# Batch norm over 64 tiles: loads of tiles 1 to 63 move from SyncE's queue to GpSimd's software queue, as one packet for each DMA engine

## The chip, the cores and the metric

The kernel runs on one core of a Trainium2 chip. The metric is the device time of one execution, in microseconds (us); the time of a kernel is the median of its runs. A profile is one execution recorded by the hardware profiler; its span is the time from its first to its last recorded event. The core has 16 DMA engines, which move data between the chip's main memory (HBM) and the core's on-chip buffer (SBUF, 128 partitions). Engines that issue or compute are named PE (TensorE), DVE (VectorE), ACT (ScalarE), POOL (GpSimd) and SP (SyncE); "SPq" and "ACTq" are the instruction queues of SP and ACT, from which DMAs are issued.

## The reference

The kernel computes an inference batch norm: each of 256 channels is scaled and shifted by constants of its own.

```python
# x: (32, 256, 128, 128) float32; gamma, beta, running_mean, running_var: (256,)
gamma * (x - mean) / np.sqrt(var + 1e-5) + beta     # each parameter as (1, 256, 1, 1)
```

x and the output are 536.87 MB each. There is one multiplication and one addition for each element that is read and written.

## The kernel before

A tile is 128 channels of one image: 128 partitions of 16,384 float32, that is 64 KB a partition and 8.39 MB in all. There are 64 tiles (`NT`), taken in order through three buffers (`NBUF`): tile i lives in buffer i % 3. A DMA of a whole tile is spread over all 16 DMA engines, eight partitions (rows of 64 KB) for each.

The parameters are fetched in four small DMAs (line 91) into `rows`, turned with a transpose and four copies on DVE, and made into `scale_t` and `shift_t` (lines 107 to 125). They are done once, at the start.

For each tile the work is split by columns: DVE does columns 0 to 14,336 (`VCOLS`), in a first piece of 2,560 (`STEP`) and a second of 11,776; ACT does the remaining 2,048. The last tile is split at 9,216 (`VLAST`). Tile 0 arrives in two halves of 8,192 columns (lines 88 and 95), and DVE's two pieces of it are 8,192 and 6,144 columns.

All order is written out by hand with semaphores, in one critical section; no scheduler moves anything:

- Loads are issued by SP (line 102). For i of 3 and more, SP first waits until the store of tile i - 3 is complete (`stored`, line 101), since that frees the buffer, and then until DVE has finished the first piece of tile i - 1 (`vdone`, line 104). So there is one load in flight at a time once the first three are through.
- DVE waits for the load of tile i (`loaded`, through `landed`) ahead of its first piece. `vdone` counts its pieces, two for each tile.
- ACT waits until both pieces of tile i are done, then until the store of tile i - 1 is complete, works on its columns (line 141), and issues the store of tile i on its own queue (line 154). So there is one store in flight at a time, up to the last two: ACT's part of the last tile waits for its load and not for the store before.
- SP ends with waits for the last store of each buffer (line 172). POOL issues nothing of the kernel's; it sets four constants before it starts.

`loaded` has one semaphore for each buffer, and every DMA adds 16 to its semaphore when it is complete. `landed(i)` gives the semaphore and the value that mean that tile i is there.

Of the kernel before, what the change touches and what calls it, by code (L numbers as in the profile page):

```python
# [8 lines left out]
NBUF = 3  # L9
# [7 lines left out]
@with_exitstack  # L17
def kernel(
    ctx: ExitStack,
    tc: tile.TileContext,  # L20
    x: bass.AP,
    gamma: bass.AP,
    beta: bass.AP,
    running_mean: bass.AP,
    running_var: bass.AP,
    out: bass.AP,
):
    nc = tc.nc
    eps = 1e-5
    f32 = mybir.dt.float32  # L30

    N, C, H, W = x.shape
    P = nc.NUM_PARTITIONS
    assert C % P == 0
    NCB = C // P
    HW = H * W
    NT = N * NCB
    B = 32
    NQ = P // B
    NE = 16  # L40
    NPAR = 4

    xr = x.rearrange("n (cb p) h w -> (n cb) p (h w)", p=P)
    outr = out.rearrange("n (cb p) h w -> (n cb) p (h w)", p=P)

    params = ctx.enter_context(tc.tile_pool(name="params", bufs=1))
    data = ctx.enter_context(tc.tile_pool(name="data", bufs=1))
    bufs = [data.tile([P, HW], f32, name=f"t{s}", tag=f"t{s}") for s in range(NBUF)]
    rows = params.tile([B, NPAR * C], f32, name="rows", tag="rows")
    turned = params.tile([B, NPAR * C], f32, name="turned", tag="turned")  # L50
    par = params.tile([P, NPAR, NCB], f32, name="par", tag="par")
    eps_t = params.tile([P, 1], f32, name="eps_t", tag="eps")
    std_t = params.tile([P, NCB], f32, name="std_t", tag="std")
    rstd_t = params.tile([P, NCB], f32, name="rstd_t", tag="rstd")
    scale_t = params.tile([P, NCB], f32, name="scale_t", tag="scale")
    ms_t = params.tile([P, NCB], f32, name="ms_t", tag="ms")
    shift_t = params.tile([P, NCB], f32, name="shift_t", tag="shift")

    loaded = [tc.alloc_semaphore(f"loaded{s}") for s in range(NBUF)]
    stored = [tc.alloc_semaphore(f"stored{s}") for s in range(NBUF)]
    early = tc.alloc_semaphore("early")
    vdone = tc.alloc_semaphore("vdone")
    adone = tc.alloc_semaphore("adone")
    fetched = tc.alloc_semaphore("fetched")
    vec = tc.alloc_semaphore("vec")
    act = tc.alloc_semaphore("act")

    with tc.tile_critical():  # L70
        count = [0]

        def step(inst, sem=None, value=None):

            if sem is not None:
                inst._wait_ge(sem, value)
            elif count[0]:
                inst._wait_ge(vec, count[0])
            inst.then_inc(vec, 1)
            count[0] += 1  # L80
            return count[0]

        left, right = slice(0, HW // 2), slice(HW // 2, HW)
        last = NT - 1

        nc.sync.dma_start(out=bufs[0][:, left], in_=xr[0][:, left]).then_inc(early, 16)
        zeroed = step(nc.vector.memset(rows[:], 0.0))  # L89
        for r, ap in enumerate((running_var, gamma, beta, running_mean)):  # L90
            inst = nc.sync.dma_start(out=rows[0:NE, r * C : (r + 1) * C], in_=ap.partition_broadcast(NE))  # L91
            if r == 0:
                inst._wait_ge(vec, zeroed)
            inst.then_inc(fetched, 16)
        nc.sync.dma_start(out=bufs[0][:, right], in_=xr[0][:, right]).then_inc(loaded[0], 16)  # L95
        for i in range(1, NT):
            s, turn = i % NBUF, i // NBUF


            if turn:  # L100
                nc.sync.wait_ge(stored[s], 16 * turn)
            inst = nc.sync.dma_start(out=bufs[s][:], in_=xr[i]).then_inc(loaded[s], 16)
            if turn:
                inst._wait_ge(vdone, 2 * (i - 1) + 1)


        step(nc.vector.memset(eps_t[:], eps))  # L107
        step(nc.vector.transpose(out=turned[:], in_=rows[:]), fetched, 16 * NPAR)  # L108

        blocks = turned.rearrange("p (rc q b) -> p rc q b", q=NQ, b=B)  # L110
        flat = par.rearrange("p r cb -> p (r cb)")
        for q in range(NQ):
            placed = step(nc.vector.tensor_copy(out=flat[q * B : (q + 1) * B], in_=blocks[:, :, q, 0]))  # L113
        var_t, gamma_t, beta_t, mean_t = (par[:, r] for r in range(NPAR))
        nc.scalar.activation(  # L115
            out=std_t[:],
            in_=var_t,
            func=mybir.ActivationFunctionType.Sqrt,
            bias=eps_t[:],
            scale=1.0,  # L120
        )._wait_ge(vec, placed).then_inc(act, 1)
        step(nc.vector.reciprocal(out=rstd_t[:], in_=std_t[:]), act, 1)  # L122
        step(nc.vector.tensor_mul(out=scale_t[:], in0=gamma_t, in1=rstd_t[:]))  # L123
        step(nc.vector.tensor_mul(out=ms_t[:], in0=mean_t, in1=scale_t[:]))  # L124
        ready = step(nc.vector.tensor_sub(out=shift_t[:], in0=beta_t, in1=ms_t[:]))  # L125
        nc.vector.wait_ge(vec, ready)

        def vector_part(i, first, end):
            t, cb = bufs[i % NBUF], i % NCB
            return nc.vector.tensor_scalar(  # L130
                out=t[:, first:end],
                in0=t[:, first:end],
                scalar1=scale_t[:, cb : cb + 1],
                scalar2=shift_t[:, cb : cb + 1],
                op0=mybir.AluOpType.mult,
                op1=mybir.AluOpType.add,
            ).then_inc(vdone, 1)

        def scalar_part(i, first):
            t, cb = bufs[i % NBUF], i % NCB  # L140
            return nc.scalar.activation(  # L141
                out=t[:, first:],
                in_=t[:, first:],
                func=mybir.ActivationFunctionType.Identity,
                bias=shift_t[:, cb : cb + 1],
                scale=scale_t[:, cb : cb + 1],
            ).then_inc(adone, 1)

        def landed(i):
            return loaded[i % NBUF], 16 * (i // NBUF + 1)  # L150

        def store(i):
            s = i % NBUF
            nc.scalar.dma_start(out=outr[i], in_=bufs[s][:])._wait_ge(adone, i + 1).then_inc(stored[s], 16)

        vector_part(0, 0, HW // 2)._wait_ge(early, 16)
        vector_part(0, HW // 2, VCOLS)._wait_ge(*landed(0))
        for i in range(1, NT):
            vector_part(i, 0, STEP)._wait_ge(*landed(i))
            vector_part(i, STEP, VLAST if i == last else VCOLS)  # L160
        for i in range(last):
            nc.scalar.wait_ge(vdone, 2 * (i + 1))
            inst = scalar_part(i, VCOLS)
            if i:
                inst._wait_ge(stored[(i - 1) % NBUF], 16 * ((i - 1) // NBUF + 1))
            store(i)
        scalar_part(last, VLAST)._wait_ge(*landed(last))
        nc.scalar.wait_ge(vdone, 2 * NT)
        store(last)

        for s in range(NBUF):
            nc.sync.wait_ge(stored[s], 16 * ((NT - s + NBUF - 1) // NBUF))
# [30 lines left out]
```

## Time and profile before

| What | Value |
|---|---|
| Time, median of 3 runs | 2484.65 us (2484.54 to 2486.47) |
| The profiled execution: its time is given as its span | 2483.3 us |
| DVE busy | 508.8 us (20%) |
| ACT busy | 139.8 us (6%) |
| POOL busy | 0.2 us |
| Bytes moved by DMA | 1073.85 MB, mean 432 GB/s |
| Chain that ended last: share of load DMAs | 93% |
| Median from issue to landing: load of a tile, store of a tile | 37.0 us, 36.5 us |

How to read the lines of a profile. A group of instructions gives the line, the engine, the operation, the tile written and the tiles read, the shapes and the count; then its busy time in us and the mean of one in ns; then the engine's idle time just before them and what ended most of it. A line of the timeline gives the start and the length in us, then the same. A line of the waits gives who waited for whom: the us in total, how often, and the longest. A line of a stretch gives the stretch, its length, the busy time of DVE, ACT and POOL in it, TensorE's clock, the mean share of the 16 DMA engines that packets take, and GB/s; a packet is booked whole in the stretch where it starts, so a short stretch can show a share above 1. A line of a DMA queue gives its packets, MB, and the time that they took as a share of 16 engines' span.

### The profile page before, as it was taken

To read this page: it belongs to the slowest core of one execution; us is meant where nothing else is said; L and a number is where in the kernel's file an instruction comes from. 1 tells how busy PE (TensorE), PEld (TensorE's weight loads), DVE (VectorE), ACT (ScalarE), POOL (GpSimd) and SP (SyncE) were. 2 spreads that over 40 slices of the span, in tenths; PEclk is the share of its full clock that TensorE was granted. 3 is DMA by queue.
4 is the path that set the end of the run, shared out by engine and by line. 5 is a ranking of instruction groups with operands and counts; after the bars stand their busy time and mean duration, and the time that the engine had idled before them with its cause. 6 is when DMAs were issued, how large, how long until landed. Compare 5 with 4: busy or idle time off the path is not lost.

```text
span 2483.3 us, 516 instructions
## 1 busy us (share of the span) xinstructions
DVE 508.8 (20%) x139; ACT 139.8 (6%) x66; POOL 0.2 (0%) x4
## 2 busy tenths in 40 slices
DVE  3122121221212212122121221212212122121220
ACT  0000000000000000000000000000000000000001
POOL 0000000000000000000000000000000000000000
DMA  9999999999999999999999999999999999999999
GB/s 415 430 439 434 428 436 436 435 433 430 432 433 438 430 432 433 435 424 437 437 428 436 438 436 429 437 435 430 436 437 436 430 437 435 429 437 435 433 433 408
DMA packets 18708, 1073.85 MB, mean 432 GB/s; under 512 B 2128, under 2 KB 2192, under 8 KB 2192
## 3 DMA queue, kind: packets, MB, share of 16 engines
q1 hardware_dynamic: 9488, 536.94, 50.1%
q10 hardware_dynamic: 9216, 536.88, 49.9%
q14 instruction: 4, 0.03, 0.0%
HBM read 536.94 MB, written 536.87 MB: 432 GB/s over the span
## 4 chain that ended last, share of the span: by engine, by line
DMA 93%; DVE 4%; another core or an unknown queue 1%; ACT 0%; issue 0%; SPq 0%; DVEq 0%
DMA t<-in_x_dram 93%; DVE t L130 4%; ACT t L141 0%; SPq L91 0%; DVE rows L89 0%; SPq L95 0%; DVE eps_t L107 0%; DVEq L198 0%; SPq L70 0%
## 5 line engine op out<-in xcount | busy, mean ns | idle before, releaser
L130 DVE TENSOR_SCALAR t<-t,scale_t,shift_t 128x11776 f32<-128x11776 f32 (+2 forms) x128 | 505.3, 3989 | 1930.4 <-DMA t<-in_x_dram 1930.2
L141 ACT ACTIVATE t<-t,shift_t,scale_t 128x2048 f32<-128x2048 f32 x64 | 138.2, 2159 | 2299.3 <-DMA out_dram<-t 2276.6
L108 DVE STREAM_TRANSPOSE turned<-rows 32x1024 f32<-32x1024 f32 x1 | 1.2, 1233 | 12.5 <-DMA rows<-in_running_mean_dram 12.5
L115 ACT ACT_TABLE_LOAD x1 | 1.3, 1283 | 0.9 <-SPq L70 0.9
L89 DVE MEMSET rows<- 32x1024 f32 x1 | 0.9, 912 | 1.2 <-SPq L70 1.2
L115 ACT ACTIVATE std_t<-par,eps_t 128x2 f32<-128x2 f32 x1 | 0.3, 296 | 14.7 <-DVE par L113 14.7
L113 DVE COPY par<-turned 32x8 f32<-32x8 f32 x4 | 0.6, 161 | 0.1
L122 DVE RECIPROCAL rstd_t<-std_t 128x2 f32<-128x2 f32 x1 | 0.2, 166 | 0.4 <-ACT std_t L115 0.4
L125 DVE TENSOR_TENSOR shift_t<-par,ms_t 128x2 f32<-128x2 f32 x1 | 0.2, 161 | 0.0
L124 DVE TENSOR_TENSOR ms_t<-par,scale_t 128x2 f32<-128x2 f32 x1 | 0.2, 161 | 0.0
L123 DVE TENSOR_TENSOR scale_t<-par,rstd_t 128x2 f32<-128x2 f32 x1 | 0.2, 160 | 0.0
L187 POOL MEMSET const-bfloat16-1.0<- 128x1 bf16 x1 | 0.1, 101 | 0.0
L187 POOL MEMSET const-uint8-127<- 128x1 uint8 x1 | 0.1, 101 | 0.0
L187 POOL MEMSET const-float32-0.0<- 128x1 f32 x1 | 0.1, 98 | 0.2 <-issue 0.2
L187 POOL MEMSET const-float32-1.0<- 128x1 f32 x1 | 0.1, 98 | 0.0
L107 DVE MEMSET eps_t<- 128x1 f32 x1 | 0.1, 59 | 0.1
## 6 DMA issues: line engine op xcount, KB each, us to landing
t<-in_x_dram SPq DMA_DIRECT2D x2, 4096.0 KB, 16.5
out_dram<-t ACTq DMA_DIRECT2D x64, 36.5
t<-in_x_dram SPq DMA_DIRECT2D x63, 37.0
rows<-in_running_var_dram SPq DMA_DIRECT2D x1, 16.0 KB, 11.3
rows<-in_gamma_dram SPq DMA_DIRECT2D x1, 16.0 KB, 11.1
rows<-in_beta_dram SPq DMA_DIRECT2D x1, 16.0 KB, 10.9
rows<-in_running_mean_dram SPq DMA_DIRECT2D x1, 16.0 KB, 11.3
```

What stands on the lines that cost most here:

```text
L89: zeroed = step(nc.vector.memset(rows[:], 0.0))
L107: step(nc.vector.memset(eps_t[:], eps))
L108: step(nc.vector.transpose(out=turned[:], in_=rows[:]), fetched, 16 * NPAR)
L113: placed = step(nc.vector.tensor_copy(out=flat[q * B : (q + 1) * B], in_=blocks[:, :, q, 0]))
L115: nc.scalar.activation(out=std_t[:], in_=var_t, func=mybir.ActivationFunctionType.Sqrt, bias=eps_t[:], scale=1.0,)._wait_ge(vec, placed).t ...
L122: step(nc.vector.reciprocal(out=rstd_t[:], in_=std_t[:]), act, 1)
L123: step(nc.vector.tensor_mul(out=scale_t[:], in0=gamma_t, in1=rstd_t[:]))
L124: step(nc.vector.tensor_mul(out=ms_t[:], in0=mean_t, in1=scale_t[:]))
L125: ready = step(nc.vector.tensor_sub(out=shift_t[:], in0=beta_t, in1=ms_t[:]))
L130: return nc.vector.tensor_scalar(out=t[:, first:end], in0=t[:, first:end], scalar1=scale_t[:, cb : cb + 1], scalar2=shift_t[:, cb : cb + 1 ...
L141: return nc.scalar.activation(out=t[:, first:], in_=t[:, first:], func=mybir.ActivationFunctionType.Identity, bias=shift_t[:, cb : cb + 1] ...
L187: nc = _bacc.Bacc("TRN2", target_bir_lowering=False, num_devices=1)
```

## The change

Loads of tiles 1 to 63 are issued by POOL, with both of their waits, and carry `single_packet=True`: the descriptors are written in software by GpSimd, and each DMA engine gets its eight rows of a tile as one packet. Tile 0's two halves and the parameters stay on SP, the stores stay on ACT's queue. Since a semaphore is now kept to one kind of issuer, the right half of tile 0 counts on a semaphore of its own (`first`), and `landed` is adapted: tile 0 waits for `first`, and the tiles of buffer 0 start their count at tile 3. The waits are for the same events as before.

```diff
@@ -61,6 +61,7 @@
     early = tc.alloc_semaphore("early")
+    first = tc.alloc_semaphore("first")
     vdone = tc.alloc_semaphore("vdone")
@@ -92,14 +93,14 @@
-        nc.sync.dma_start(out=bufs[0][:, right], in_=xr[0][:, right]).then_inc(loaded[0], 16)
+        nc.sync.dma_start(out=bufs[0][:, right], in_=xr[0][:, right]).then_inc(first, 16)
         for i in range(1, NT):
             s, turn = i % NBUF, i // NBUF
             if turn:
-                nc.sync.wait_ge(stored[s], 16 * turn)
-            inst = nc.sync.dma_start(out=bufs[s][:], in_=xr[i]).then_inc(loaded[s], 16)
+                nc.gpsimd.wait_ge(stored[s], 16 * turn)
+            inst = nc.gpsimd.dma_start(out=bufs[s][:], in_=xr[i], single_packet=True).then_inc(loaded[s], 16)
             if turn:
                 inst._wait_ge(vdone, 2 * (i - 1) + 1)
@@ -147,7 +148,9 @@
         def landed(i):
-            return loaded[i % NBUF], 16 * (i // NBUF + 1)
+            if i == 0:
+                return first, 16
+            return loaded[i % NBUF], 16 * (i // NBUF + (1 if i % NBUF else 0))
```

## The prediction

> **What bounds the kernel now.** I read the page first: busy shares, the row of DMA shares, the queues, the chain, the costliest groups and the DMA issues.
>
> ```profile
> span 2483.3 us, 516 instructions
> ...
> DVE 508.8 (20%) x139; ACT 139.8 (6%) x66; POOL 0.2 (0%) x4
> ...
> DMA  9999999999999999999999999999999999999999
> ...
> q1 hardware_dynamic: 9488, 536.94, 50.1%
> q10 hardware_dynamic: 9216, 536.88, 49.9%
> ...
> DMA 93%; DVE 4%; another core or an unknown queue 1%; ACT 0%; issue 0%; SPq 0%; DVEq 0%
> ...
> L130 DVE TENSOR_SCALAR t<-t,scale_t,shift_t 128x11776 f32<-128x11776 f32 (+2 forms) x128 | 505.3, 3989 | 1930.4 <-DMA t<-in_x_dram 1930.2
> L141 ACT ACTIVATE t<-t,shift_t,scale_t 128x2048 f32<-128x2048 f32 x64 | 138.2, 2159 | 2299.3 <-DMA out_dram<-t 2276.6
> ...
> out_dram<-t ACTq DMA_DIRECT2D x64, 36.5
> t<-in_x_dram SPq DMA_DIRECT2D x63, 37.0
> ```
>
> The 16 DMA engines are full in every slice; DVE and ACT mostly wait for them. Loads (q1) and stores (q10) take half each. The store queue has 9,216 packets for 64 stores on 16 engines: nine for each store and engine, which are its eight rows of 64 KB and a ninth that I take for the completion. 49.9% of 16 x 2483.3 us over 8,192 rows makes 2.42 us a row. A load or a store has eight rows on an engine, 19.3 us if it had the engine alone; it takes 37, so the queues share each engine.
>
> Then the timeline, two periods in the middle, and the waits of the queue that issues the loads:
>
> ```profile
> 901.56 7.93 DVE L130 TENSOR_SCALAR t<-t,scale_t,shift_t 128x2560 f32<-128x2560 f32 x2 [30.74 <-DMA t<-in_x_dram]
> 903.20 77.69 SPq L102 DMA_DIRECT2D t<-in_x_dram  x3
> 925.68 2.09 ACT L141 ACTIVATE t<-t,shift_t,scale_t 128x2048 f32<-128x2048 f32 x1 [36.55 <-DMA out_dram<-t]
> 927.81 0.34 ACTq L154 DMA_DIRECT2D out_dram<-t  x1
> 940.19 7.94 DVE L130 TENSOR_SCALAR t<-t,scale_t,shift_t 128x2560 f32<-128x2560 f32 x2 [30.69 <-DMA t<-in_x_dram]
> ```
> ```profile
> SPq L101 <- DMA out_dram<-t: 1398.1, 61, 68.8
> SPq L102 <- DVE t L130: 985.0, 61, 16.2
> ```
>
> A load lands at 901.56, DVE's first piece (1.62 us of the 7.93) frees the next load, issued at 903.20; the next lands at 940.19: a period of 38.63 us. A store ends at 925.68, ACT works 2.09 us, and the next store is issued at 927.81. So each stream has a break, but the breaks are some 20 us apart, and the other stream fills the engines. The second view says why: the load's wait for a free buffer (L101) ends about 16 us before the wait for DVE (985.0 over 61). Last, stretches of the trace:
>
> ```profile
> 1.60:1.80 0.20, 0.20 (x1) 0.20 (x1) 0.00 (x0) 1.00 0.00 0
> 1.80:2.00 0.20, 0.20 (x1) 0.20 (x1) 0.00 (x0) 1.00 2.94 819
> ...
> 2.40:2.60 0.20, 0.00 (x0) 0.00 (x0) 0.00 (x0) 1.00 1.00 328
> 16.00:22.00 6.00, 5.28 (x10) 0.30 (x1) 0.00 (x0) 1.00 1.01 437
> 1000.00:1038.63 38.63, 7.94 (x2) 2.09 (x1) 0.00 (x0) 1.00 1.00 434
> 2465.00:2470.00 5.00, 0.00 (x0) 0.00 (x0) 0.00 (x0) 1.00 1.00 433
> 2479.00:2479.50 0.50, 0.00 (x0) 0.00 (x0) 0.00 (x0) 1.00 0.60 262
> ```
>
> The last two columns are DMA share and GB/s; a packet is booked where it starts. Loads alone (16 to 22) run at 437 GB/s, stores alone (2465 to 2470) at 433, both together at 434. So the engines are the limit in any mixture: order costs nothing, only empty engines cost. The first load, issued at 0.95, has its first row at about 1.95: **1.0 us** from issue to data on a free queue, and the 16th engine starts about 0.6 us after the first. The last rows start at 2479.0 to 2479.5 (two of 64 KB), end 2.42 us later, and the last store, issued at 2454.70, lands 26.9 us on, at 2481.6: the completion adds almost nothing when nothing is ahead of it.
>
> The sum of before: 64 periods of 38.63 make 2472.3; start 1.95; after the last landing 1.7; the remaining 7.3 are small irregularities. Span 2483.3, which lies 1.35 below the median of 2484.65, so I add 1.35 at the end.
>
> **The change, part by part.** (1) 63 issues leave SP (0.33 us each) and come to POOL, which has nothing but four memsets; SP's remaining work is its closing waits. Off the path, except through the start of each load. (2) The waits on `stored` and `vdone` move with them; POOL has only later loads queued behind. No wait is added. (3) The semaphore `first` renames tile 0's wait: nothing. (4) Each engine gets a load as one packet of eight rows. If an engine changes queues between packets only, a load holds it for 19.3 us while the store stands still. Following that from a landing: the next load starts some 5 us later (DVE 1.62 and a start of 1 to 3 us), in which the store gets about two of its eight rows; then the load takes everything for 19.3 us. Loads thus run ahead, until after two or three tiles they stand at `stored`. From then on one event, the end of store i-3, releases both load i and ACT's work for store i-2. The load goes through first (19.3), then the store (19.3), and its end is again the only event. **The two breaks now coincide, and nothing fills them.**
>
> The price of a break g, per tile, is the earlier of two starts, plus 0.6 us for the last engine:
> - Store: ACT 2.09 + 0.03 + 1.0 from issue to data = 3.1 us. This is an upper bound, however slow the software queue is: rows of the store then go first, and the load takes its 19.3 us among them.
> - Load: two waits and the writing of descriptors in software. The trace has no such issue. Low end: the hardware queue's 1.0 us. High end: 3.1, where the store decides.
>
> So g is 1.6 to 3.7. I take the middle for the load's start, 2.05, since neither row is nearer: software should not beat 1.0, and 3.1 is a cap rather than a measurement. g = **2.7**. A gain is excluded here, because before pays nothing for its breaks. [...]
>
> It occurs at the ends of stores 0 to 60: 61 x 2.7 = **165**. After store 61 no load is left: 3.1 + 0.6 = **3.7**, then the last two stores back to back (ACT's 6.4 us for the last tile lies beside store 62).
>
> (5) The head. Loads 1 and 2 no longer queue behind tile 0 on SP; POOL issues both at about 1 us, so their packets start after one or two 32 KB rows of tile 0 (1.21 us each). An engine then does load 1 (to about 23), one half row, load 2 (to 43.6), and the remaining 13 half rows and the parameters, to 59.3. DVE's second piece (3.48), ACT (2.09) and the start (1.0) bring the first store to about 66. Empty engines: **6.7 us**; none, if POOL's first issue came after tile 0 (at 21 us or later).
>
> Sum: 2472.3 + 1.95 + 6.7 + 164.7 + 3.7 + 1.7 + 7.3 = 2658.4; with 1.35, **2660 us**. Bounds: 61 x 1.6 gives 2593, 61 x 3.7 gives 2721; without the empty head 7 less.
>
> [...] The row first: in before, neither queue overtakes the other, both 37 us for 19.3 us of rows. [...]
>
> **The rivals.**
> - *Not faster, not slower: rows still alternate.* If single-packet changes nothing in the sharing, each stream's breaks stay covered by the other, and POOL's slower start too. For it: the engines stay full with breaks of 1.65 and 2.5 us now. Against: the packet is the unit that the queue counts suggest. 2485 to 2490.
> - *Rows alternate, and DVE keeps POOL from writing descriptors.* A load is then released after DVE's first piece, just as the 11776-column piece starts (7.93 - 1.62 = 6.3 us). It starts 1.62 + 6.3 + 2.65 = 10.6 us after a landing, the store 7.93 + 2.1 + 1.6 = 11.6 after it; both wait for the same landing, and about 9.5 us per tile are empty: 2485 + 61 x 9.5 = 3065. For it: DVE is busy exactly then. In my forecast it costs nothing, since the restart comes 19.3 us after the landing and DVE ends at 7.93. [...]
> - *Loads from the software queue run at a lower rate.* The lowest inner slice has 424 GB/s and the two at the edges 408 to 415, against 434. At 408 a load takes 20.6 instead of 19.3 us: 1.23 x 64 = 79 more, 2739.
> - *Faster.* If eight rows in one packet saved what lies between rows, loads could run at the 439 GB/s of the best slice: 64 x 19.3 x (1 - 434/439) = 14 us, 2471. It decides only if g is under 14 / 61 = 0.23 us, but the fastest start in the trace is 1.0.
>
> **How the numbers follow.** Packets held whole, breaks coincide: 0.74. Lower rate on top: 0.06. Alternating rows with starved descriptors: 0.10. Alternating rows, hidden: 0.06. Faster: 0.04. The measurement tells 0.2% from no change, 5 us. The range, 2570 to 2800, holds the first case with its bounds and a head or irregularities that cost nothing (2593 less 14 is 2579), and the second with its price; 0.80 together. Faster 0.04; within 0.2% 0.04 (two thirds of the hidden case); slower 0.92.
>
> **What would show it.** Right: the period goes from 38.6 to about 41.3 us; a load takes about 22 us from issue to landing and a store about 39 (19 of them behind the load); the rate falls from 434 to about 406 GB/s (434 x 38.6 / 41.3), with empty stretches of 2 to 4 us right after each store; the load's wait is for the store, not for DVE. Wrong: loads still at 37 us mean rows still alternate; then a period of 38.6 means a hidden change, one near 48 with idle from landing to DVE's end means starved descriptors. Full engines, but a longer period, mean a lower rate. If the period is right, but the load starts later than the next store, the software start is longer than 3.1 us and g sits at its cap.

## The result, and the profile after

The changed kernel takes 3035.56 us (median of 4 runs, 3033.64 to 3038.01) against 2485.52 us (also 4 runs): a ratio of 1.2216, 95% interval 1.2201 to 1.2231. The forecast was 2660 us, between 2570 and 2800. The second of the rivals had given 3065.

The page of the changed kernel, the lines that answer to those shown of before:

```profile
span 3031.9 us, 519 instructions
DVE 508.6 (17%) x139; ACT 139.8 (5%) x66; POOL 369.7 (12%) x67
...
DMA  8999788888879888797987989888797988889787
...
q0 software_dynamic: 9072, 528.49, 43.5%
q10 hardware_dynamic: 9216, 536.88, 40.9%
...
L103 POOL DMA_DIRECT2D t<-in_x_dram x63 | 369.5, 5866 | 2588.8 <-DVE t L131 2458.1
L142 ACT ACTIVATE t<-t,shift_t,scale_t 128x2048 f32<-128x2048 f32 x64 | 138.2, 2159 | 2818.2 <-DVE t L131 2621.3
...
out_dram<-t ACTq DMA_DIRECT2D x64, 40.2
t<-in_x_dram POOLq DMA_DIRECT2D x63, 45.7
```

Three things are new. The DMA engines are no longer full. POOL is busy for 5.87 us in the mean for each load that it issues (line 103). And ACT, which waited for its own stores before, now waits for DVE. The load queue has 9,072 packets for 63 loads on 16 engines: still nine each, eight rows of 64 KB and one of 4 bytes. So the trace does not show the one packet of eight rows that the change asks for.

One period in the timeline, and what POOL waited for:

```profile
1037.62 7.94 DVE L131 TENSOR_SCALAR t<-t,scale_t,shift_t 128x2560 f32<-128x2560 f32 x2 [39.71 <-DMA t<-in_x_dram]
1039.53 6.15 POOL L103 DMA_DIRECT2D t<-in_x_dram  x1 [41.50 <-DVE t L131]
1045.65 2.09 ACT L142 ACTIVATE t<-t,shift_t,scale_t 128x2048 f32<-128x2048 f32 x1 [45.55 <-DVE t L131]
1047.77 0.34 ACTq L157 DMA_DIRECT2D out_dram<-t  x1
1085.65 7.93 DVE L131 TENSOR_SCALAR t<-t,scale_t,shift_t 128x2560 f32<-128x2560 f32 x2 [40.10 <-DMA t<-in_x_dram]
```
```profile
POOL t L103 <- DVE t L131: 2458.1, 59, 42.8
POOL t L103 <- DMA out_dram<-t: 129.7, 2, 87.3
```

A load lands at 1037.62. DVE's first piece (1.62 us) frees the next load, and POOL begins to issue it at 1039.53. It is done at 1045.68, just when DVE ends its second piece (1037.62 + 7.94 = 1045.56). ACT needs DVE's end too, so the store is issued at 1047.77. Both streams now start from one event, the landing. The landings from 177.74 to 2998.40 are 59 periods of 47.81 us in the mean; before it was 38.63.

Stretches of this period (DMA share and GB/s are the last two columns; a row is booked where it starts):

```profile
1037.62:1040.00 2.38, 2.38 (x2) 0.00 (x0) 0.47 (x1) 1.00 0.07 28
1040.00:1041.00 1.00, 1.00 (x1) 0.00 (x0) 1.00 (x1) 1.00 0.00 0
1041.00:1046.00 5.00, 4.55 (x1) 0.35 (x1) 4.67 (x1) 1.00 0.00 0
1046.00:1048.00 2.00, 0.00 (x0) 1.74 (x1) 0.00 (x0) 1.00 1.48 524
1037.62:1085.65 48.03, 7.93 (x2) 2.09 (x1) 6.15 (x1) 1.00 0.84 351
```

One row of 64 KB, the last of the store, begins soon after the landing (28 GB/s for 2.38 us); then no row begins until 1046.38. In the packet records all 16 engines are empty from 1040.12 to 1046.38; in the mean an engine is empty for 7.5 us of the 48.

The trace also records each packet's start and length, which lets the whole difference be added up. For each instant between the first row and the end of the last, the engines of the 16 without a row were counted ("empty"). "Rows' excess" is the time by which rows took longer than the usual 2.418 us (1.209 for a row of 32 KB). Both are given as the mean of one engine.

| | span, us | empty | rows' excess | span over before | (empty + excess) over before |
|---|---|---|---|---|---|
| before | 2483.3 | 2.1 | 5.2 | | |
| changed | 3031.9 | 448.5 | 102.1 | 548.6 | 543.3 |

5.0 of the 5.3 us that are missing lie at the end: SP, which closes the program, waits 5.0 us for POOL there, and did not before.

```profile
SPq L71 <- POOLq L71: 5.0, 1, 5.0
```

Nearly all of the excess sits in two rows of each load: in the median its first row takes 3.10 us and its second 3.35, all others 2.42.

### The profile page after: what moved, and what is told of

It reads as the page before. It is cut to its first block, busy times and chain, and to the rows that moved or that the text cites. A ratio compares the mean times of both kernels' runs of the same rounds, so it can differ in the third digit from the quotient of the medians.

```text
span 3031.9 us, 519 instructions
## 1 busy us (share of the span) xinstructions
DVE 508.6 (17%) x139; ACT 139.8 (5%) x66; POOL 369.7 (12%) x67
## 3 DMA queue, kind: packets, MB, share of 16 engines
q0 software_dynamic: 9072, 528.49, 43.5%
## 4 chain that ended last, share of the span: by engine, by line
DMA 94%; DVE 4%; issue 1%; ACT 0%; another core or an unknown queue 0%; SPq 0%; DVEq 0%; POOLq 0%
DMA t<-in_x_dram 91%; DVE t L131 3%; DMA out_dram<-t 2%; DMA rows<-in_running_mean_dram 1%; ACT t L142 0%; DVE turned L109 0%; SPq L92 0%; DVE rows L90 0%; DVE par L114 0%; ACT std_t L116 0%; DVE rstd_t L123 0%; DVE ms_t L125 0%; DVE scale_t L124 0%; DVE shift_t L126 0%
## 5 line engine op out<-in xcount | busy, mean ns | idle before, releaser
L103 POOL DMA_DIRECT2D t<-in_x_dram x63 | 369.5, 5866 | 2588.8 <-DVE t L131 2458.1
```

Source lines behind the costliest of these rows:

```text
L103: inst = nc.gpsimd.dma_start(out=bufs[s][:], in_=xr[i], single_packet=True).then_inc(loaded[s], 16)
```

## The experiments

**Is it the packet form or DVE?** Theory A: rows of loads and stores alternate in any case, and DVE's long piece holds GpSimd's issue. Theory B: software descriptors in one packet are slow or late in themselves. Four runs tell them apart.

The packet form taken away:

```diff
-            inst = nc.gpsimd.dma_start(out=bufs[s][:], in_=xr[i], single_packet=True).then_inc(loaded[s], 16)
+            inst = nc.gpsimd.dma_start(out=bufs[s][:], in_=xr[i]).then_inc(loaded[s], 16)
```

> The changed kernel without the one-packet form: GpSimd still issues the loads, in the default packets. Theory A (DVE's 11,776-column piece keeps GpSimd from writing descriptors, rows of loads and stores alternate in any case): GpSimd's issue still takes about 6.2 us and ends with DVE's piece, the period stays at 47.5 to 48 us, time 3035 within 15. Theory B (the one-packet form itself makes the loads late or slow): without it the period falls back to about 38.6 us, time 2485 to 2510. A mixture would lie between.

3038.62 us, ratio 1.2216 (1.2198 to 1.2234), the same as with it. The issue took 6.14 us and there were again 9,072 packets. The one-packet form changes nothing that the trace shows.

DVE made to wait until POOL has issued:

```diff
+            nc.gpsimd.memset(mark[:, i : i + 1], 0.0).then_inc(wrote, 1)      # behind the issue of load i
...
-            vector_part(i, STEP, VLAST if i == last else VCOLS)
+            inst = vector_part(i, STEP, VLAST if i == last else VCOLS)
+            if i < last:
+                inst._wait_ge(wrote, i + 1)
```

> The changed kernel, and DVE begins its second piece of tile i only after GpSimd has issued the load of tile i+1 and written a mark behind it. Theory A: the issue takes 0.5 us as it did where DVE was idle, the load's first rows come about 3.5 us after a landing instead of 9.2, DVE's second piece starts about 1 us later than before, the streams' breaks no longer coincide, period 38.6 to 39 us, time 2485 to 2510. Theory B (one packet or software descriptors are late or slow in themselves): the issue or the start stays long with DVE idle, time above 2800.

2786.91 us, ratio 1.1199 (1.1177 to 1.1221): neither. The timeline of this run:

```profile
1041.57 1.61 DVE L134 TENSOR_SCALAR t<-t,scale_t,shift_t 128x2560 f32<-128x2560 f32 x1 [33.28 <-DMA t<-in_x_dram]
1044.00 2.10 ACT L145 ACTIVATE t<-t,shift_t,scale_t 128x2048 f32<-128x2048 f32 x1 [41.21 <-DMA out_dram<-t]
1044.52 0.53 POOL L105 DMA_DIRECT2D t<-in_x_dram  x1 [42.67 <-DMA out_dram<-t]
1045.04 0.12 POOL L108 MEMSET mark<- 128x1 f32 x1
1045.19 6.41 DVE L134 TENSOR_SCALAR t<-t,scale_t,shift_t 128x11776 f32<-128x11776 f32 x1 [2.00 <-POOL mark L108]
1046.12 0.34 ACTq L160 DMA_DIRECT2D out_dram<-t  x1
```

The issue takes 0.53 us where DVE is idle, as theory A says. But the time did not come back: load and store now both wait for the end of a store (1044.00). Half of the loss remains. What POOL waited for:

```profile
POOL t L105 <- DMA out_dram<-t: 2653.0, 61, 87.2
```

A late release on the hardware queue, in the kernel before:

```diff
-                inst._wait_ge(vdone, 2 * (i - 1) + 1)
+                inst._wait_ge(vdone, 2 * i)
```

> The kernel before (hardware queue on SyncE), but a load is released by DVE's second piece of the tile before instead of by the first: the load is issued at landing + 7.95 us and its rows come 1.0 us later, 8.95 against 9.15 in the changed kernel. Theory A with the loss in the late release (after some tiles load and store wait for one landing): period 47.5 to 48, time 2990 to 3030. If the slow first two rows after the idle (3.1 and 3.4 us instead of 2.42) belong to the software queue and not to any restart, 1.7 us per tile less: about 2920. Theory B (the software queue or the one packet is what costs): 2485 to 2500.

3047.9 us, ratio 1.2258 (1.224 to 1.2276). No software queue is in this kernel, and it loses as much as the changed one: 469.5 us empty and 100.8 of rows' excess. The estimate was 18 us short of it. The slow first rows are there too (3.13 and 3.35 us), so they belong to a load's restart and not to the software queue.

DVE's second piece in a form with two tensor inputs:

```diff
-            vector_part(i, STEP, VLAST if i == last else VCOLS)
+            one_port_part(i, STEP, VLAST if i == last else VCOLS)
...
+        def one_port_part(i, first, end):
...      # nc.vector.scalar_tensor_tensor: t * scale_t + shift_t, which is broadcast over the columns
```

> The changed kernel with DVE's second piece computed in an operation with two tensor inputs (scale in one operand, the shift broadcast as the other), about 12.3 us instead of 6.4. [...] Theory A in the form that any DVE work blocks GpSimd: the issue takes 12 us, the period grows by about 6 us, 3300 to 3420. Theory B: 3035 or more.

2782.07 us, ratio 1.1187 (1.117 to 1.1204). DVE works for 12.48 us instead of 6.41, and POOL issues meanwhile in 0.53 us:

```profile
1082.58 12.48 DVE L142 SCALAR_TENSOR_TENSOR t<-t,scale_t,shift_t 128x11776 f32<-128x11776 f32 x1
1083.44 2.09 ACT L153 ACTIVATE t<-t,shift_t,scale_t 128x2048 f32<-128x2048 f32 x1 [40.93 <-DMA out_dram<-t]
1083.96 0.53 POOL L103 DMA_DIRECT2D t<-in_x_dram  x1 [42.50 <-DMA out_dram<-t]
```

So it is not DVE's being busy that holds POOL, but the form of the instruction: POOL's issue takes 6.15 us beside `tensor_scalar` (6.41 us for the piece) and 0.53 us beside this form (12.48 us). If the form decides, an issue of about 0.5 us and a time of 2485 to 2510 us had been expected: the issue is so, the time is not. "One-port" is only the kernel's name for this form, after its function; the traces show the times and who waits, and no port. And the same 300 us are left:

```profile
POOL t L103 <- DMA out_dram<-t: 2653.8, 61, 86.9
```

**Where do the other 300 us come from?** In both runs all 61 waits of POOL end with a store. Theory C: this is set at the start. Loads 1 and 2 no longer queue behind tile 0, so all three buffers are full before the first store begins; its end then releases a load and a store together, and so does each later one. Theory D: the software queue costs it.

The start alone, on the hardware queue of the kernel before (the right half of tile 0 goes behind loads 1 and 2):

```diff
-        nc.sync.dma_start(out=bufs[0][:, right], in_=xr[0][:, right]).then_inc(loaded[0], 16)
         for i in range(1, NT):
...
+            if i == 2:
+                nc.sync.dma_start(out=bufs[0][:, right], in_=xr[0][:, right]).then_inc(loaded[0], 16)
```

> The kernel before, all loads on SyncE's hardware queue and released as before; only the order at the start is changed: the right half of tile 0 is issued behind loads 1 and 2, so that the first store begins when all three buffers are full, as in the changed kernel. Theory C (what was left in the runs with an unhindered GpSimd, 300 us, is set at the start: the first store's end releases a load and a store at once, and the breaks then coincide for good): load and store both wait for the store's end, the break is 1.1 us to the load's first row, 0.6 for the last engine and 1.6 for two slow rows, 3.3 a tile, 61 x 3.3 = 200, and some 7 us empty at the start: 2690, between 2650 and 2760. Theory D (the software queue itself costs those 300 us): 2485 to 2500.

2722.63 us, ratio 1.0964 (1.0948 to 1.0981): one DMA moved at the start costs 240 us. SP's waits of this run:

```profile
SPq L100 <- DMA out_dram<-t: 2605.2, 61, 83.2
```

All 61 loads wait for a store and none for DVE, where before each had waited for a store and then 16 us more for DVE.

The start mended, in the run where DVE waits for POOL and in the one-port run:

```diff
+            if i == 1:
+                nc.gpsimd.wait_ge(first, 16)
```

> The run in which DVE's second piece waits for GpSimd's issue, with one more edit: GpSimd issues load 1 only when tile 0 has landed, so that the first store falls into the middle of load 2 as in the kernel before. Theory C: the breaks stay apart, period 38.6 to 38.9, time 2485 to 2510. Theory D: 2780 as without the edit.

> The run with DVE's second piece in one-port form (12.5 us), with the start mended in the same way. Theory C: 2485 to 2510. Theory D: 2780 as without the edit.

2503.52 us, ratio 1.0084 (1.0069 to 1.0099), and 2503.25 us, 1.0083 (1.0066 to 1.01). The first of them:

```profile
1031.32 1.61 DVE L136 TENSOR_SCALAR t<-t,scale_t,shift_t 128x2560 f32<-128x2560 f32 x1 [29.65 <-DMA t<-in_x_dram]
1033.23 0.53 POOL L107 DMA_DIRECT2D t<-in_x_dram  x1 [38.00 <-DVE t L136]
1033.75 0.12 POOL L110 MEMSET mark<- 128x1 f32 x1
1033.90 6.41 DVE L136 TENSOR_SCALAR t<-t,scale_t,shift_t 128x11776 f32<-128x11776 f32 x1 [0.97 <-POOL mark L110]
1045.79 2.09 ACT L147 ACTIVATE t<-t,shift_t,scale_t 128x2048 f32<-128x2048 f32 x1 [36.59 <-DMA out_dram<-t]
1047.92 0.34 ACTq L162 DMA_DIRECT2D out_dram<-t  x1
1070.12 1.61 DVE L136 TENSOR_SCALAR t<-t,scale_t,shift_t 128x2560 f32<-128x2560 f32 x1 [29.81 <-DMA t<-in_x_dram]
```
```profile
1031.32:1070.12 38.80, 8.03 (x2) 2.09 (x1) 0.64 (x2) 1.00 1.01 436
```

A load's issue (1033.23) and a store's (1047.92) are 14.7 us apart, the engines are full at 436 GB/s, and the period is 38.8 us. Theory C holds; of theory D's 300 us at most 18 are left. The span is 18.1 us longer than before: 5.3 us empty and 7.6 of rows' excess more than before, and 5.0 at the end for POOL, 17.9 together. The empty time comes from the edit and not from the queue: 5.3 us of it lie between 20 and 60 us, where load 1 is held back until tile 0 has landed. What causes the excess was not tested.

The start mended, POOL still held by DVE:

> The changed kernel with the start mended in the same way, and GpSimd's issue still held by DVE. If holding the issue brings load and store to one landing whatever the start was, as the late release on the hardware queue did with the start of before: 3010 to 3045. If the start decides here too: under 2800.

3045.18 us, ratio 1.2265 (1.2246 to 1.2283). All 61 waits of POOL end with DVE, as in the mended runs, but an issue takes 6.01 us in the mean here against 0.57 there:

```profile
L105 POOL DMA_DIRECT2D t<-in_x_dram x63 | 378.8, 6012 | 2592.1 <-DVE t L133 2568.8 <-DMA t<-in_x_dram 23.3
```

A late issue pulls load and store to one landing with either start, so the two causes do not add.

**When does DVE let go?** The first piece enlarged, with the same end:

```diff
-STEP = 2560
+STEP = 8192
```

> The changed kernel with one size changed: DVE's first piece is 8,192 columns instead of 2,560 (4.55 us instead of 1.62), the second 6,144 (3.48 us). The load is released 2.9 us later after a landing, but DVE ends at the same 8.0 us. If the end of DVE's running instruction sets when GpSimd can write, the issue shrinks to about 3.2 us and ends where it did: 3020 to 3050. If the release set the start, 2.9 us more a tile: 3210.

3041.78 us, ratio 1.2228 (1.2208 to 1.2249). POOL's issue takes 3.21 us and ends with DVE's 3.47 us piece again:

```profile
1042.54 7.94 DVE L131 TENSOR_SCALAR t<-t,scale_t,shift_t 128x8192 f32<-128x8192 f32 x2 [39.70 <-DMA t<-in_x_dram]
1047.38 3.21 POOL L103 DMA_DIRECT2D t<-in_x_dram  x1 [44.42 <-DVE t L131]
```

The end of DVE's instruction sets the start, not the release. Last, the second piece in eight instructions, with the start mended:

```diff
-            vector_part(i, STEP, VLAST if i == last else VCOLS)
+            part = ((VLAST if i == last else VCOLS) - STEP) // PIECES      # 1,472 columns; PIECES is 8
+            for k in range(PIECES):
+                vector_part(i, STEP + k * part, STEP + (k + 1) * part)
...      # the values waited for on vdone follow
```

> The changed kernel with the mended start and DVE's second piece cut into 8 instructions of 1,472 columns (about 0.85 us each), released after the first piece as before. [...]

2525.75 us (2506.52 to 2541.09), ratio 1.0158 (1.0096 to 1.0221). The median issue takes 0.78 us (0.53 to 3.32) and starts under DVE's work:

```profile
1031.49 9.27 DVE L137 TENSOR_SCALAR t<-t,scale_t,shift_t 128x2560 f32<-128x2560 f32 x9 [30.08 <-DMA t<-in_x_dram]
1033.40 0.78 POOL L109 DMA_DIRECT2D t<-in_x_dram  x1 [38.56 <-DVE t L137]
```

So the hold lasts for one instruction, and POOL gets in between two. Expected were 2500 to 2515 us if it lasts for one instruction, and 3045 if it lasts over a run of them; the median lies 11 us above the first, and the four runs spread over 35 us. The profiled one, 2514.30 us, has a span 11.1 us longer than the mended run's, and 10.9 of it are rows' excess (23.7 us against 12.7); why these rows are slow is not known.

Nothing that was run beats the kernel before. Between its first row and its last only 7.3 us are empty engines or slow rows (the table above).

## Why the prediction was wrong

- *What bounds the kernel: right in the main.* "Only empty engines cost": empty engines are 446.4 of the 548.6 us, and 5.0 lie at the end; but 96.9 are rows that are slow after a pause, which the forecast had at nothing. (One reading was loose: the two issues shown, at 903.20 and 927.81, are 24.6 us apart and not some 20. Nothing rests on it.)
- *Part 4, "a load holds it for 19.3 us while the store stands still": this is the step that failed.* From the end of POOL's issue to the landing a load takes 40.0 us (1045.68 to 1085.65), and 36.4 in the mended run (1033.76 to 1070.12). The forecast had about 22. In the packet records of the period shown the load's rows start every 4.83 us from the third on, with the store's rows between them. That an engine stays with one queue for all eight rows was the author's assumption: no run shows it, nor the 2.7 us a tile (164.7 us of the sum) that rest on it. What the runs show in its place: the eight rows issued with the one-packet flag are eight packets on record and alternate as such, and the period grew by 9.18 us a tile (47.81 against 38.63). No run here has a packet of several such rows.
- *Part 4, the price of the load's start.* It was bounded by 1.0 and 3.1 us. In the changed kernel it is 1.91 from the landing to POOL's start (1.62 of it DVE's first piece), 6.15 for the issue, and 0.70 to the first row, at 1046.38: 8.76 in all, and 9.1 in the mean of the 16 engines. The upper bound rested on the store going first if the load is late; but once the load is late, the store hangs on the same landing. That DVE would long be idle at the restart held only with a load that keeps the store standing.
- *Rival 2: right in what holds the load, given 0.10, and its time is in part luck.* It put the load's start at 10.6 us after a landing, 9.5 us empty for each tile, 3065. Measured: a start at 9.1 us, a period longer by 47.81 - 38.63 = 9.18, 3035.6. But only 7.2 us a tile are empty (446.4 less 7.3 at the start, over 61); the slow rows, which it did not have, make another 1.6. That DVE's piece holds POOL's issue agrees with the traces as far as the piece is a long `tensor_scalar`: the issue took 0.53 us with DVE idle, 6.15 beside the 6.41 us piece, 3.21 beside the 3.47 us piece, and 0.53 beside the form with two tensor inputs.
- *Breaks that coincide at a store's end: right as a mechanism, but not what the changed kernel does.* The forecast's 2660 assumed a held packet for it. With alternating rows it came about in three runs (2782, 2787, 2723), from the start alone. The break was sized at 2.7 us. In the run in which DVE waits (2787) 3.1 us a tile are empty (201.2 us in all, less the 2.1 of before and 7.3 at the start, over 61); the terms left out are the two slow rows, 1.6 us a tile, and the 5.0 us at the end. A load released by a store's end lands 2.4 us before the next store ends (1041.57 and 1044.00), so that the next load must wait for a store again, and so on to the end.
- *Part 5, the start: right in size, wrong in weight.* It put the first store at about 66 us and 6.7 us of empty engines; the store was issued at 68.64, and 7.3 us were empty. The 6.7 us were booked once. Its effect on the order of everything behind it was worth 240 to 300 us in the three runs in which nothing else fixed that order (2723, 2782 and 2787 us).
- *Rival 1, "rows still alternate" with every break covered, 2485 to 2490.* With the two causes removed it is 2503: covered but for 18 us, 5.3 of them from the mended start itself. Rows do alternate, so its first half was right and its conclusion missed both causes.

## What to carry to other kernels

Where two streams fill the DMA engines, ask of each break not only how long it is but which event starts it: breaks of 1.65 and 2.5 us cost nothing apart in the kernel before (2.1 us empty in 2483), breaks that fell together cost 240 to 300 us in three runs, and a single transfer moved at the start decided which (2723 us). Before loads go to GpSimd's queue, look at what DVE runs at the moment of the issue: one long `tensor_scalar` held the issue to its end (6.15 us, 3.21 beside a shorter one), and a wait of DVE for the issue (0.53 us), the form with two tensor inputs (0.53) or shorter pieces (0.78) let it through. With the issue free and the start mended the software queue still gained nothing: 2503 us against 2483. When a forecast rests on an assumption that no trace shows, price the combination in which it fails, and ask what in the trace would make it fail.

## What the runs showed of the hardware that was not expected

- The one-packet form of a GpSimd load of eight 64 KB rows for each engine left no mark: nine packets for each engine and load with and without it, rows that alternate with the other queue's, 3035.6 and 3038.6 us.
- After a pause of all 16 engines the first two rows of a load take 3.10 and 3.35 us instead of 2.42, on the hardware queue (3.13 and 3.35) as on the software queue. A store does not show it: the first rows of the changed kernel's first store, after a pause of some 7 us, take 2.46 us. Why is open.
- The kernels that issue from GpSimd's queue close 5.0 us later: SP waits for POOL at the end, in all nine traces with such loads and in none of the three without.
